# First stage of a two-layer diffusion backbone: by quarters of the features, with two engines' order written out

## The chip, the cores and the metric

The kernel runs on one core of a Trainium2 chip. The metric is the device time of one execution in microseconds (us). Five engines each work through an instruction list of their own: TensorE (PE, matrix products), VectorE (DVE), ScalarE (ACT), GpSimd (POOL) and SyncE (SP), which here issues nearly all loads. They wait for each other through semaphores; a load is done by 16 DMA engines.

## The reference, cut to what matters

The change touches the start of layer 0 alone. There, 768 tokens (512 latent, 256 context) of 1024 features are normalised, shifted and scaled by a modulation that comes from the condition vectors, and projected by one wide matrix:

```python
m_lat = jnp.split((sc @ mod_w[l] + mod_b[l])[:, None, :], 6, axis=-1)      # sc = silu(c)
m_ctx = jnp.split((scc @ mod_w[l] + mod_b[l])[None, None, :], 6, axis=-1)  # scc = silu(c_ctx)
h_ctx = _modulate(_rms(x_ctx, norm_pre_mix[l]), m_ctx[0], m_ctx[1])        # h * (1 + scale) + shift
h_lat = _modulate(_rms(x_lat, norm_pre_mix[l]), m_lat[0], m_lat[1])
gq, gk, gv, gog, gz, aq, ak, av = _split(h @ w_in, EVEN_SIZES)             # 256 256 512 512 32 512 128 128
logit = (z @ gla_w_gate[d] + gla_b_gate[d])                                # z: halves of gz
g = log_sigmoid(logit) / 16                                                # forget gates of the linear attention
```

Parts 0 and 1 of the modulation (shift and scale) are wanted at once. Parts 2 and 3 are wanted after the mixer; parts 4 and 5 later. Then come gated linear attention, attention with rotary positions, an output projection, a feed-forward layer, and a second layer of the same build.

## The kernel before, in words

Every fp32 product is made from three products of a rounded operand H and its remainder L (`mm3`): H·H, H·L and L·H. A weight is loaded to `raw`, rounded by ScalarE into `wH` and subtracted by VectorE into `wL`; the activations get the tiles `x` (H and L) in the same way. Wide tiles of 1024 columns in PSUM (`mm_tile`, two buffers) take projections, 512-column ones (`sc0`, `sc1`, and `tr` with two buffers) take small results and transposes.

The first stage (`run`, L1655 to L1709) loads six token tiles, normalises them, and has TensorE transpose them into `xT` (features on the partitions). Then the modulation's parts 0 and 1 are summed by TensorE in two halves of 512 features: eight loads of 512 KB to a half, 32 products per half (`mod_acc`), a copy (`modrows`), a transpose (`modT`), and a column for each feature (`modcol`, `aff`). With these, VectorE and ScalarE scale `xT` and split it. Only with all 1024 features there does the first projection begin (z and the first half of the attention's queries, 288 columns, tiles `nat`).

After that TensorE's order is written out: `run("qk0 qk0 e m ...")` names generators, and each name advances one of them by a step; `pin` keeps those instructions in that order, while VectorE, ScalarE and SyncE are ordered by the scheduler's own estimates. The names are `qk0` (queries and keys of the linear attention, `gqk0` and `gqk2`), `v0` (its values), `q` (the other half of the attention's queries), `kv`, `e` (the forget gates: z turned to `zT`, products `logit`, then `am` and `glaf`) and `m` (`mod_vec`, L531). A step of `m` loads 512 KB of `mod_w` and has VectorE add it, times a condition value, to two running sums `macc` (latent and context). Eight steps make the pair of part 2, eight more the pair of part 3; each pair ends with `mod_acc` on TensorE (a sum over the partitions), `modrows`, `modT` and `modcol`. Behind these stands the gated linear attention (`c0`, `l0`, tiles `arrg`, `pcg`). Its inputs are `gqk0`, `gqk2` and `glaf`.

Of the kernel before, what the change touches and what calls it, by code (L numbers as in the profile page):

```python
# [17 lines left out]
P = 128  # L18
# [321 lines left out]
class Net:  # L340
# [3 lines left out]
    def __init__(self, ctx, tc, I, out):  # L344
        self.tc, self.nc, self.I, self.out = tc, tc.nc, I, out
        tc.nc.scalar.preload_act_table_set("silu_and_others")
        self.side = 0
        self.whole = False
        self.pinned = False
# [38 lines left out]
    def constants(self):  # L388
# [11 lines left out]
        self.col_rows(  # L400
            "rows", 0, P, (
# [6 lines left out]

        nc.gpsimd.memset(self.scT, 0.0)
        nc.scalar.activation(  # L410
            self.scT[:, :, 0:2].rearrange("p k r -> p r k"),
            self.col[:, R_C : R_C + 16].rearrange("p (r k) -> p r k", r=2),
            AF.Silu,
        )
        self.modcol, self.gates = {}, {}

    def col_rows(self, nm, r0, r1, parts):

        rows = self.wp.tile([P, WU], F32, tag="mraw", bufs=2, name=nm)[: r1 - r0, :P]
        for at, src, n in parts:  # L420
            self.nc.scalar.dma_start(out=rows[at - r0 : at - r0 + n, :], in_=src)
        pt = self.tr_tile(f"pt_{nm}")
        self.tr(pt[:, 0 : r1 - r0], rows, self.ident[0 : r1 - r0, 0 : r1 - r0])
        self.nc.vector.tensor_copy(self.col[:, r0:r1], pt[:, 0 : r1 - r0])

    def late_constants(self):
        nc, I, cst = self.nc, self.I, self.cst
        self.col_rows(
            "rows2", R_NQM, R_END, (
# [10 lines left out]
        mf = self.wp.tile([P, WU], F32, tag="mraw", bufs=2, name="masks_f")[:, :160].rearrange("p (m i) -> p m i", m=5)  # L440
        nc.scalar.dma_start(out=mf, in_=I["const_masks"])
        nc.vector.tensor_copy(self.masks, mf)
# [30 lines left out]
    def mod_loads(self, l, ms, k, pool, bufs):  # L473
        us = []
        for m in ms:
            u = (pool or self.wp).tile([P, WU], F32, tag="mraw", bufs=bufs, name=f"mraw{l}{m}{k}")
# [54 lines left out]
    def mod_vec(self, pool, jobs, own=None, bufs=2, sums=2, single=False):  # L531
# [4 lines left out]
        load = lambda l, k, m: self.mod_loads(l, (m,), k, own, bufs)[0]  # L536
        u = load(*steps[0])
        i = 0
        for l, ms, then in jobs:
            self.mod_tiles(l, [m for m, r in ms if r == 0])  # L540
            accs = [pool.tile([P, D], F32, tag="macc", bufs=sums, name=f"macc{l}{m}{r}") for m, r in ms]
            while i < len(steps) and steps[i][0] == l and steps[i][2] in [m for m, _ in ms]:
                k, m = steps[i][1:]
                i += 1
                ahead = load(*steps[i]) if i < len(steps) else None
                here = [(a, r) for a, (mm, r) in zip(accs, ms) if mm == m]
                for x, (a, r) in enumerate(here):
# [3 lines left out]
                    if k == 0:  # L551
                        nc.vector.tensor_scalar(a, u, w, None, op0=ALU.mult)
                    else:
                        nc.vector.scalar_tensor_tensor(a, u, w, a, op0=ALU.mult, op1=ALU.add)  # L554
                u = ahead
# [63 lines left out]
    def rstd(self, ss, n, w=1, f=1.0):  # L619
        nc = self.nc  # L620
        ms = self.sm.tile([P, w], F32, tag=f"ms{w}", name="ms")
        nc.vector.tensor_scalar(ms, ss, f / n, f * EPS, op0=ALU.mult, op1=ALU.add)  # L622
# [4 lines left out]
    def sumsq(self, src, junk=None, ss=None):  # L627
# [4 lines left out]
        self.nc.scalar.activation(junk, src, AF.Square, accum_out=ss)  # L632
# [55 lines left out]
    def unit(self, src, k, n, pool=None, to=None):  # L688
# [10 lines left out]
        nc.scalar.copy(H[:, :m], raw[:, :m])  # L699
        nc.vector.tensor_tensor(L[:, :m], raw[:, :m], H[:, :m].bitcast(F32), op=ALU.subtract)  # L700
# [357 lines left out]
    def even_mixer(self, h, mix, zu, last):  # L1058
# [14 lines left out]
        gqk = [mixg.tile([P, NT], F32, tag=f"gqk{x}", bufs=1, name=f"gqk{2 * x}") for x in range(2)]  # L1073
        og = [p.tile([P, NTT, 256], F32, name=f"og{c}") for c, p in enumerate((mixg, mix))]
        tp = self.open_pool("gate")
        zn = tp.tile([P, NTT, 32], F32, name="zn")
        zT = tp.tile([32, NT], F32, name="zT")

        def ev_z(t0, pt):
            nc.scalar.copy(zn[:, t0 : t0 + 2, :], pt[:, :, 0:32])  # L1080
            nc.scalar.copy(q_part(0)[:, t0 : t0 + 2], pt[:, :, 32:288].rearrange("p t (m e) -> p t m e", m=4))

        with self.tc.issue_after(last):
            self.gemm_nat(w, 1536, 288, h, tiles, ev_z, us=zu)

# [7 lines left out]
        def decays():  # L1093
            for g in range(0, NTT, 4):
                pt = self.tr_tile("zTp")
                n = min(4, NTT - g)
                for i in range(n):
                    self.tr(pt[0:32, i * P : (i + 1) * P], zn[:, g + i, :], self.ident)
                nc.vector.tensor_copy(zT[:, g * P : (g + n) * P], pt[0:32, : n * P])
            yield  # L1100
            for c in range(2):
                yield from self.gla_gates(mixg, tp, c, zT, wg, fs[c])
# [3 lines left out]
        mods = self.mod_vec(tp, ((0, ((2, 0), (2, 1)), (2, R_NQM)), (0, ((3, 0), (3, 1)), None)), tp, 3, 4)  # L1106

        def nat(c0, evac):

            us = self.nat_units(w, c0, 256, 0) + self.nat_units(w, c0, 256, 1)  # L1110
# [5 lines left out]
        def ev_q(t0, pt):  # L1116
            nc.scalar.copy(q_part(1)[:, t0 : t0 + 2], pt[:, :, :256].rearrange("p t (m e) -> p t m e", m=4))
# [4 lines left out]
        gq, gk, ends = {}, {}, {}  # L1122
        def qk(c):
            Ws = {x: self.unit_cols(w, x * P) for x in (c, c + 2)}
            yield
            for x in (c, c + 2):
                pt = self.mm_tile(f"gqk{x}")
                for g in groups:
                    self.gemm_T(pt, Ws[x], h, (g,))
                    if g is groups[-1]:  # L1130
                        t = gqk[x // 2] if c == 0 else mixg.tile([P, NT], F32, tag=f"gqk{x // 2}", bufs=1, name=f"gqk{x}")
# [732 lines left out]
```

## Time and profile before

| | |
|---|---|
| median of three runs | 1747.95 us (1745.9 to 1750.31) |
| the profiled execution | 1749.34 us, span of its instructions 1747.5 us |
| TensorE busy | 1700.9 us, 97% of the span |
| VectorE, ScalarE, GpSimd busy | 1280.9, 857.8, 74.2 us |
| granted TensorE clock, mean | 0.993 of full speed |
| DMA | 187.23 MB, 107 GB/s over the span |

The span runs from the first to the last instruction, and all times in the rows below count from its start. The page cuts it in 40 slices of 43.7 us; only the first slice has TensorE below nine tenths (six), and only it and the next one have the DMA engines at seven tenths or more:

```profile
PE   6999999999999999999999999999999999999998
DVE  5879658735966979787668658787764678878785
...
PEclk8999999999999999999999999999999999999999
DMA  8731013154322424332234752121114333233333
```

A busy TensorE is not TensorE at its peak: a row of the timeline gives the count of merged instructions, and the distance between the starts of equal rows is what one costs.

### The profile page before, as it was taken

What the parts mean: (1) busy time and instruction counts of PE and PEld (TensorE: products, weight loads), DVE (VectorE), ACT (ScalarE), POOL (GpSimd) and SP (SyncE); (2) the same over time, 40 slices, a digit from 0 to 9 for tenths busy, and PEclk for the clock granted to TensorE, in tenths of its full rate; (3) what the DMA queues carried; (4) which work ended last, traced back from release to release, by engine and by line L of the source; (5) the groups of instructions that cost most, each with busy time, mean ns of one, the idle gap of its engine ahead of it and who ended that gap; (6) DMA issues with size and microseconds to landing.
All of it is one profiled execution on the core that took longest, in us unless ns stands there. A gap on an engine that the chain in (4) does not pass through costs nothing. (4 is left out here: it accounts for less than half of the span.)

```text
span 1747.5 us, 32790 instructions
## 1 busy us (share of the span) xinstructions
PE 1700.9 (97%) x13732; PEld 1526.0 (87%) x13732; DVE 1280.9 (73%) x2036; ACT 857.8 (49%) x1473; POOL 74.2 (4%) x93
## 2 busy tenths in 40 slices
PE   6999999999999999999999999999999999999998
PEld 4889986788999989989998988889898899989997
DVE  5879658735966979787668658787764678878785
ACT  5545557746543333333347336666644664344342
POOL 1004100001000000000001000000000100000000
PEclk8999999999999999999999999999999999999999
DMA  8731013154322424332234752121114333233333
GB/s 318 222 112 39 3 39 107 36 156 139 113 90 73 153 77 156 109 110 61 73 123 143 262 160 63 48 62 50 50 62 133 121 98 108 86 102 106 99 106 120
DMA packets 169647, 187.23 MB, mean 107 GB/s; under 512 B 6262, under 2 KB 140956, under 8 KB 169500
## 3 DMA queue, kind: packets, MB, share of 16 engines
q1 hardware_dynamic: 167568, 181.56, 32.8%
q10 hardware_dynamic: 1932, 3.59, 0.7%
q8 instruction: 107, 1.75, 0.4%
q14 instruction: 40, 0.33, 0.1%
HBM read 175.66 MB, written 9.46 MB: 106 GB/s over the span
## 5 line engine op out<-in xcount | busy, mean ns | idle before, releaser
L371 PE MATMUL nat<-wH,x 128*128 128x256 f32 (+1 forms) x1216 | 229.0, 287 | 0.4 <-issue 0.4
L754 ACT CAST wH<-raw 128x1024 fp32r<-128x1024 f32 x120 | 124.5, 1051 | 197.2 <-PE acc L371 86.2
L700 DVE TENSOR_TENSOR wL<-raw,wH 128x1024 fp32r<-128x1024 f32 (+1 forms) x126 | 151.3, 1206 | 84.3 <-ACT wH L699 83.9
L371 PEld LDWEIGHTS nat<-wH,x 128*128 128x128 f32 x1216 | 193.3, 193 | 3.8 <-ACT y L1329 0.8
L755 DVE TENSOR_TENSOR wL<-raw,wH 128x1024 fp32r<-128x1024 f32 x120 | 145.2, 1221 | 64.9 <-ACT wH L754 64.8
L699 ACT CAST wH<-raw 128x1024 fp32r<-128x1024 f32 (+1 forms) x126 | 128.9, 1038 | 127.8 <-PE nat L371 34.4
L371 PE MATMUL nat<-wL,x 128*128 128x256 f32 (+1 forms) x608 | 173.4, 285 | 0.0
L371 PE MATMUL acc<-wH,gH 128*128 128x512 f32 x440 | 171.8, 390 | 0.0
L371 PE MATMUL acc<-wH,gL 128*128 128x512 f32 x440 | 171.5, 390 | 0.0
L371 PE MATMUL acc<-wL,gH 128*128 128x512 f32 x440 | 171.5, 390 | 0.0
L847 DVE TENSOR_TENSOR y<-y,acc 128x1024 f32<-128x1024 f32 x135 | 115.2, 863 | 37.0 <-PE acc L371 32.8
L554 DVE SCALAR_TENSOR_TENSOR macc<-mraw,scT,macc 128x1024 f32<-128x1024 f32 x98 | 122.6, 1277 | 10.7 <-DMA mraw<-in_mod_w_dram 10.4
L371 PE MATMUL ff<-x,wH 128*128 128x512 f32 (+1 forms) x512 | 127.6, 340 | 0.0
L624 POOL TENSOR_TENSOR rs<-ms,neghalf 128x1 f32<-128x1 f32 (+2 forms) x62 | 58.0, 937 | 1543.2 <-DVE ms L622 1543.1
L371 PEld LDWEIGHTS nat<-wL,x 128*128 128x128 f32 x608 | 117.3, 193 | 0.0
L371 PE MATMUL oproj<-wH,x 128*128 128x512 f32 x320 | 102.5, 397 | 3.2 <-ACT x L1270 3.2
L371 PEld LDWEIGHTS acc<-wH,gL 128*128 128x128 f32 x440 | 82.6, 188 | 17.3
L371 PEld LDWEIGHTS acc<-wH,gH 128*128 128x128 f32 x440 | 82.7, 188 | 16.6
L371 PEld LDWEIGHTS acc<-wL,gH 128*128 128x128 f32 x440 | 82.7, 188 | 16.5
L371 PEld LDWEIGHTS ff<-x,wH 128*128 128x128 f32 x512 | 87.3, 190 | 10.1
L955 ACT COPY qkh<-arr 128x512 f32<-128x512 f32 x112 | 70.1, 642 | 36.3 <-DVE arr L960 32.1
L371 PE MATMUL ff<-x,wL 128*128 128x256 f32 (+1 forms) x256 | 86.2, 337 | 0.0
(344 smaller groups left out, 4047.2 us busy)
## 6 DMA issues: line engine op xcount, KB each, us to landing
mraw<-in_mod_w_dram SPq DMA_DIRECT2D x96, 512.0 KB, 4.8
raw<-in_ffn_w_gate_dram SPq DMA_DIRECT2D x44, 512.0 KB, 3.7
raw<-in_ffn_w_up_dram SPq DMA_DIRECT2D x44, 512.0 KB, 3.8
raw<-in_ffn_w_down_dram SPq DMA_DIRECT2D x44, 512.0 KB, 3.6
raw<-in_odd_w_in_dram SPq DMA_DIRECT2D x40, 512.0 KB, 3.7
raw<-in_even_w_in_dram SPq DMA_DIRECT2D x16, 512.0 KB, 4.6
x<-xr SPq DMA_DIRECT2D x14, 512.0 KB, 2.6
xr<-x SPq DMA_DIRECT2D x14, 512.0 KB, 8.1
```

Source lines behind the costliest of these rows:

```text
L371: return self.pin(self.nc.tensor.matmul(*a, **k))
L554: nc.vector.scalar_tensor_tensor(a, u, w, a, op0=ALU.mult, op1=ALU.add)
L624: nc.gpsimd.tensor_tensor(rs, ms, self.neghalf.to_broadcast([P, w]), op=ALU.pow)
L699: nc.scalar.copy(H[:, :m], raw[:, :m])
L700: nc.vector.tensor_tensor(L[:, :m], raw[:, :m], H[:, :m].bitcast(F32), op=ALU.subtract)
L754: self.nc.scalar.copy(H, f)
L755: self.nc.vector.tensor_tensor(L, f, H.bitcast(F32), op=ALU.subtract)
L847: nc.vector.tensor_tensor(y, y, pt, op=ALU.add)
L955: nc.scalar.copy(qkv[:, :, :, half, :], dst)
```

## The change

The first stage is rewritten around quarters of 256 features (`begin`, new). Of each quarter, the modulation's parts 0 and 1 are loaded (four loads of 512 KB), summed by TensorE into `md` (32 products of 128 columns), turned, and used to scale and split that quarter of `xT`. At once TensorE multiplies that quarter by its rows of the weights for `gqk0`, `gqk2` and the values: three projections are open in PSUM at the same time and grow by a quarter each (both `mm` buffers, both `sc` and one `tr` buffer). Per quarter the order on TensorE is: context tokens of all three, the sums of the next quarter's modulation, latent tokens. z is made by small fp32 products in spare columns of `gqk0`'s PSUM tile (`gates`, 16 products after the second quarter and 16 in the fourth). The attention's first queries get a projection of their own (`Q`, 256 columns).

Within the first stage, VectorE's and ScalarE's instructions are pinned as TensorE's are. The steps of `mod_vec` are pinned too: it loads three steps ahead instead of one, from four buffers instead of three, and its first seven steps are written at the end of the third quarter (three) and in the fourth (two and two). The remaining nine are in the plan as `m`. The late constants go through SP's queue instead of ACT's, ahead of the third quarter's loads, and ScalarE's first table load stands behind its first four loads. A norm's input tiles live in a pool of their own (`xr`), whose buffers the modulation's loads and sums take over.

```diff
-    def mod_vec(self, pool, jobs, own=None, bufs=2, sums=2, single=False):
+    def mod_vec(self, pool, jobs, own=None, bufs=2, sums=2, single=False, tags=("macc", "mraw"), deep=1):
...
-        u = load(*steps[0])
+        us = [load(*x) for x in steps[:deep]]
...
-                        nc.vector.scalar_tensor_tensor(a, u, w, a, op0=ALU.mult, op1=ALU.add)
+                        self.pin(nc.vector.scalar_tensor_tensor(a, u, w, a, op0=ALU.mult, op1=ALU.add))
...
+    def begin_loads(self, pp, q):
+        us = []
+        for i in range(2):
+            u = pp.tile([P, 4, 2, 256], F32, tag="mraw", bufs=5, name=f"mraw0{q}{i}")
+            src = self.I["mod_w"][0, 512 * i : 512 * i + 512, 0:2048].rearrange("(k p) (m f) -> p k m f", p=P, m=2)
+            for m in (1, 0):
+                self.nc.sync.dma_start(out=u[:, :, m], in_=src[:, :, m, 256 * q : 256 * q + 256])
+            us.append(u)
+        return us
+
+    def begin_weights(self, q):
...
+        for at, c0, n in ((0, 0, 128), (128, 256, 128), (256, 512, 256)):
+            nc.sync.dma_start(out=rv[:, :, at : at + n], in_=w[:, :, c0 : c0 + n])
+
+        def split():
+            self.pin(nc.scalar.copy(H, raw))
+            self.pin(nc.vector.tensor_tensor(L, raw, H.bitcast(F32), op=ALU.subtract))
...
+    def begin(self, pp, xr, h, xT, us, ws):
...
+        def columns(q, rows, md):
...
+            for r, tok in ((1, slice(512, 768)), (0, slice(0, 512))):
+                for k in range(ks.start, ks.stop):
+                    x = xT[:, k, tok]
+                    if k % 2:
+                        self.pin(nc.scalar.activation(x, x, AF.Identity, bias=shift[:, r, k : k + 1], scale=A[:, r, k : k + 1]))
+                    else:
+                        self.pin(nc.vector.tensor_scalar(x, x, A[:, r, k : k + 1], shift[:, r, k : k + 1], op0=ALU.mult, op1=ALU.add))
+                H, L = h.hl(ks, tok)
+                self.pin(nc.scalar.copy(H, xT[:, ks, tok]))
+                self.pin(nc.vector.tensor_tensor(L, xT[:, ks, tok], H.bitcast(F32), op=ALU.subtract))
...
+        for q in range(4):
+            if q < 2:
+                us[q + 2] = self.begin_loads(pp, q + 2)
+                split[q + 2] = self.begin_weights(q + 2)
+            if q == 2:
+                mods = self.mod_vec(
+                    xr, ((0, ((2, 0), (2, 1)), (2, R_NQM)), (0, ((3, 0), (3, 1)), None)), xr, 4, 2, tags=("x1", "x0"), deep=3
+                )
+            if q == 3:
+                self.held = True
+                wq = [self.nat_units(I["even_w_in"][0], 1568, 256, half)[0] for half in range(2)]
+                self.held = False
+            across(q, 0, ctx)
+            across(q, 1, ctx)
+            values(q, 4)
+            if q in (1, 2):
+                rows = sums(q + 1, us[q + 1], md)
+            if q == 3:
+                gates(range(4, 8))
+                for _ in range(2):
+                    next(mods)
+            across(q, 0, lat)
+            if q == 0:
+                rows = sums(1, us[1], md)
+            if q in (1, 2):
+                columns(q + 1, rows, md)
+            across(q, 1, lat)
+            if q == 0:
+                columns(1, rows, md)
+            if 1 <= q + 1 < 3:
+                ws[q + 2] = split[q + 2]()
+            values(q, 0)
+            values(q, 2)
+            if q == 1:
+                gates(range(4))
+            if q == 2:
+                for _ in range(3):
+                    next(mods)
+            if q == 3:
+                for _ in range(2):
+                    next(mods)
+        return qk, v, wq, mods, late
...
+        for g in range(4):
+            self.pin(nc.vector.tensor_copy(zT[:, 192 * g : 192 * g + 192], pq[32 * g : 32 * g + 32, 768:960]))
+        nc.scalar.mul(gqk[0], pq[:, :NT], 0.125)
+        nc.scalar.copy(gqk[1], pk[:, :NT])
...
-        run("qk0 qk0 e m qk0 e e v0 qk0 e e m qk0 e e m v0 e e m m q v0 m m v0 m m kv q m m q m q m m m m m m m m m qk1 kv m")
+        run("Q m m Q e e m Q m e e m Q m q e e m q m e e q m m q m kv m kv m m m")
+        for _ in mods:
+            pass
         tp.release()
+        xr.release()
         gp = self.open_pool("gla")
-        run("c0 l0 kv m c0 kv c0 v1 qk1 c0 p p qk1 c0 l0 p qk1 l0 c0 g0 qk1 l0 p c1 p v1 l0 p v1 l0 c1 p v1 l0 c1 l1 g1 g0 c1 g0 r0 c1 l1 r0 g0 l1")
+        run("c0 l0 qk1 kv c0 kv c0 v1 qk1 c0 p p qk1 c0 l0 p qk1 l0 c0 g0 qk1 l0 p c1 p v1 l0 p v1 l0 c1 p v1 l0 c1 l1 g1 g0 c1 g0 r0 c1 l1 r0 g0 l1")
```

How the instructions move is shown at two places. The first is VectorE where z is copied out of PSUM (`zT`), from which the forget gates start. In the list of before, with the sums `macc` of the part-2 pair around it:

```order
L554 SCALAR_TENSOR_TENSOR macc020_691<-mraw023_845,scT_79,macc020_691 128x1024
L554 SCALAR_TENSOR_TENSOR macc021_692<-mraw023_845,scT_79,macc021_692 128x1024
L554 SCALAR_TENSOR_TENSOR macc020_691<-mraw024_918,scT_79,macc020_691 128x1024
L700 TENSOR_TENSOR wL_749<-raw_747,wH_748 128x1024
L1099 COPY zT_466<-zTp_678 32x512
L1099 COPY zT_466<-zTp_684 32x256
L554 SCALAR_TENSOR_TENSOR macc021_692<-mraw024_918,scT_79,macc021_692 128x1024
```

And in the changed list, where `col` and `masks` are the late constants, `lb_tmp` the lower bounds of layer 1, and `wL` the remainders of weights for projections still to come:

```order
L570 SCALAR_TENSOR_TENSOR macc021_710<-mraw025_719,scT_78,macc021_710 128x1024
L570 SCALAR_TENSOR_TENSOR macc020_709<-mraw026_775,scT_78,macc020_709 128x1024
L570 SCALAR_TENSOR_TENSOR macc021_710<-mraw026_775,scT_78,macc021_710 128x1024
L431 COPY col_83<-pt_rows2_854 128x86
L454 CAST masks_278<-masks_f_279 128x160
L464 TENSOR_TENSOR lb_tmp_863<-col_83 128x16
L716 TENSOR_TENSOR wL_1106<-raw_1104,wH_1105 128x1024
L1261 COPY zT_844<-gqk0_338 32x192 x4
L467 TENSOR_TENSOR lb_tmp_863<-col_83,lb_tmp_863 128x2x8 x2
L716 TENSOR_TENSOR wL_1112<-raw_1110,wH_1111 128x1024
```

Before, nine of the pair's 16 sums stand ahead of `zT`. Now 14 do, of which three are shown, with two weight remainders among them and a third right before `zT`; only the eighth step follows.

The second place is TensorE, where the forget gates' products `logit` stand. Before, they stand between two parts of a projection:

```order
L371 MATMUL gqk0_653<-x2_313,wL_643 128x256
L371 MATMUL logit00_723<-zT_466,wg_620 128x256
L371 MATMUL logit01_732<-zT_466,wg_620 128x256
L371 MATMUL gqk2_753<-x0_311,wH_648 128x512
L371 MATMUL gqk2_753<-x1_312,wH_648 128x512
L371 MATMUL gqk2_753<-x0_311,wL_649 128x512
```

Now they stand behind the first tile of the attention's queries (`nat_883`, whose last two products are shown), and the sum over the partitions of the part-2 pair (`mod_acc`) follows at once, ahead of the second tile (`nat_959`):

```order
L370 MATMUL nat_883<-wL_731,x2_324 128x256
L370 MATMUL nat_883<-wH_730,x3_325 128x256
L370 MATMUL logit00_934<-zT_844,wg_858 128x256
L370 MATMUL logit01_943<-zT_844,wg_858 128x256
L370 MATMUL mod_acc_952<-macc020_709,one_81 32x512 x2
L370 MATMUL mod_acc_952<-macc021_710,one_81 32x512 x2
L370 MATMUL nat_959<-wH_724,x0_322 128x256
L370 MATMUL nat_959<-wL_725,x0_322 128x256
```

Before, `mod_acc` of this pair stood behind all eight `logit` products and three more tiles. Now it stands between the second and the third of those products. In the changed program `logit` waits for the four copies `zT`, `mod_acc` for the eighth step's sums, and the transposes behind `nat_959` for the copy `modrows` of `mod_acc`.

## Rows read from the trace of the kernel before

**Rows 1.** Busy time by stretch: start:end, length, busy us (count) by engine, PEclk, DMA share, GB/s

```profile
20.00:30.00 10.00, 7.06 (x84) 3.15 (x83) 6.38 (x19) 5.29 (x11) 0.52 (x1) 0.91 1.06 388
30.00:40.00 10.00, 8.11 (x52) 3.72 (x53) 5.17 (x15) 4.00 (x8) 0.00 (x0) 0.50 0.75 251
...
124.00:151.00 27.00, 27.00 (x403) 25.34 (x402) 26.53 (x77) 17.96 (x45) 13.29 (x8) 1.00 0.25 75
151.00:180.00 29.00, 28.83 (x625) 26.48 (x624) 27.03 (x68) 16.38 (x34) 11.23 (x12) 1.00 0.07 21
```

**Rows 2.** Timeline of TensorE, 8 to 61: start us, us, engine, line, operation, count [idle before]

```profile
8.41 1.92 PE L374 MATMUL xT<-ident,xt 128*128 128x128 f32 x8
...
22.00 2.36 PE L371 MATMUL mod_acc<-mraw,scT 128*32 128x256 f32 x38
...
32.97 1.08 PE L371 MATMUL mod_acc<-mraw,scT 128*32 128x256 f32 x8 [0.27 <-DMA mraw<-in_mod_w_dram]
...
37.63 0.59 PE L371 MATMUL nat<-wH,x 128*128 128x288 f32 x1
...
59.60 0.62 PE L371 MATMUL gqk<-x,wH 128*128 128x512 f32 x2
...
60.29 0.62 PE L371 MATMUL gqk<-x,wH 128*128 128x512 f32 x2
```

**Rows 3.** Timeline of ScalarE and VectorE in the first stage

```profile
4.55 1.06 ACT L632 ACTIVATE junk<-xt 128x1024 bf16<-128x1024 f32 x1 [2.54 <-DMA xt<-in_ctx_dram]
...
24.41 0.42 DVE L485 COPY modrows<-mod_acc 128x256 f32<-128x256 f32 x1 [1.62 <-DMA mraw<-in_mod_w_dram]
...
25.43 0.37 DVE L497 TENSOR_TENSOR modcol<-modT,col 128x4 f32<-128x4 f32 x4 [0.59 <-PE modT L374]
...
30.84 0.81 ACT L1703 ACTIVATE xT<-xT,modcol,aff 128x512 f32<-128x512 f32 x1
...
31.68 0.62 ACT L665 CAST x<-xT 128x512 fp32r<-128x512 f32 x1
...
32.33 0.69 DVE L666 TENSOR_TENSOR x<-xT,x 128x512 fp32r<-128x512 f32 x1 [0.23 <-ACT x L665]
```

**Rows 4.** Timeline of ScalarE, copies behind two neighbouring tiles of a projection

```profile
115.10 0.59 ACT L1117 COPY natq<-nat 128x512 f32<-128x512 f32 x1 [8.33 <-PE nat L371]
...
120.95 0.59 ACT L1117 COPY natq<-nat 128x512 f32<-128x512 f32 x1 [0.39 <-PE nat L371]
```

**Rows 5.** Timeline of VectorE, ScalarE and TensorE, operations that the steps below price

```profile
48.76 1.28 ACT L1104 ACT_TABLE_LOAD   x1 [0.26 <-issue]
...
60.13 0.17 DVE L466 TENSOR_SCALAR nlb<-lb 128x16 f32<-128x16 f32 x1
...
66.74 1.00 DVE L1099 COPY zT<-zTp 32x512 f32<-32x512 f32 x2
...
67.99 1.13 PE L371 MATMUL logit<-zT,wg 32*128 32x256 f32 x4
...
81.59 1.22 DVE L700 TENSOR_TENSOR wL<-raw,wH 128x1024 fp32r<-128x1024 f32 x1
...
81.70 0.78 ACT L1136 COPY gqk<-gqk 128x768 f32<-128x768 f32 x1
...
85.00 0.75 DVE L552 TENSOR_SCALAR macc<-mraw,scT 128x1024 f32<-128x1024 f32 x1
...
93.56 7.25 DVE L554 SCALAR_TENSOR_TENSOR macc<-mraw,scT,macc 128x1024 f32<-128x1024 f32 x6
...
120.85 1.06 PE L371 MATMUL mod_acc<-macc,one 128*32 128x512 f32 x8
```

**Rows 6.** Timeline of VectorE and TensorE where the gated-attention stage begins

```profile
123.72 0.42 DVE L1248 TENSOR_TENSOR arrg<-gqk,glaf 128x256 f32<-128x256 f32 x1
...
128.05 0.36 PE L371 MATMUL nat<-wH,x 128*128 128x256 f32 x1
...
152.60 0.29 DVE L1025 COPY Sg<-pdg 128x128 f32<-128x128 f32 x1 [1.59 <-PE pdg L371]
```

More of the change, by code (lines that the diff above doesn't have):

```diff
@@ L540, in mod_vec @@
             self.mod_tiles(l, [m for m, r in ms if r == 0])
-            accs = [pool.tile([P, D], F32, tag="macc", bufs=sums, name=f"macc{l}{m}{r}") for m, r in ms]
+            accs = [pool.tile([P, D], F32, tag=tags[0], bufs=sums, name=f"macc{l}{m}{r}") for m, r in ms]
             while i < len(steps) and steps[i][0] == l and steps[i][2] in [m for m, _ in ms]:
                 k, m = steps[i][1:]
+                if i + deep < len(steps):
+                    us.append(load(*steps[i + deep]))
                 i += 1
-                ahead = load(*steps[i]) if i < len(steps) else None
+                u = us.pop(0)
                 here = [(a, r) for a, (mm, r) in zip(accs, ms) if mm == m]
@@ L1073, in even_mixer @@
         gqk = [mixg.tile([P, NT], F32, tag=f"gqk{x}", bufs=1, name=f"gqk{2 * x}") for x in range(2)]
+        (pq, pk), pv, wq, mods, late = begun
         og = [p.tile([P, NTT, 256], F32, name=f"og{c}") for c, p in enumerate((mixg, mix))]
         tp = self.open_pool("gate")
-        zn = tp.tile([P, NTT, 32], F32, name="zn")
         zT = tp.tile([32, NT], F32, name="zT")
[L1079 to L1084, printed above, removed]
+        for g in range(4):
+            self.pin(nc.vector.tensor_copy(zT[:, 192 * g : 192 * g + 192], pq[32 * g : 32 * g + 32, 768:960]))
+        nc.scalar.mul(gqk[0], pq[:, :NT], 0.125)
+        nc.scalar.copy(gqk[1], pk[:, :NT])
+        for t0 in tiles:
+            nc.scalar.copy(gv[:, t0 : t0 + 2, 0:256], pv[t0])
+        late()
         wg = tp.tile([32, 2, 256], F32, name="wg")
@@ L1114, in nat, with queries, ev_q @@
                 yield
-        def ev_q(t0, pt):
-            nc.scalar.copy(q_part(1)[:, t0 : t0 + 2], pt[:, :, :256].rearrange("p t (m e) -> p t m e", m=4))
+        def queries(n, us=None):
+            def ev_q(t0, pt):
+                nc.scalar.copy(q_part(n)[:, t0 : t0 + 2], pt[:, :, :256].rearrange("p t (m e) -> p t m e", m=4))
+            return nat(1536 + 32 + 256 * n, ev_q, us)
         def ev_kv(t0, pt):
             nc.scalar.copy(natk[:, t0 : t0 + 2, :], pt[:, :, :256])
-        gq, gk, ends = {}, {}, {}
+        gq, gk, ends = {0: gqk[0]}, {0: gqk[1]}, {}
         def qk(c):
@@ L1707, in run @@
-            zu += self.nat_units(I["even_w_in"][0], 1536, 288, 1)
-            self.late_constants()
+                    self.pin((nc.vector.tensor_copy if hf else nc.scalar.copy)(dst, pt.rearrange("p (k i) -> p k i", k=4)))
+            norm(order[0])
+            norm(order[1])
+            scaled(order[0])
+            for i, t in enumerate(order):
+                if i + 2 < len(order):
+                    norm(order[i + 2])
+                if i + 1 < len(order):
+                    scaled(order[i + 1])
+                turn(t)
+                if i == 1:
+                    finish()
@@ L1710, in ender @@
+            begun = self.begin(pp, xr, h, xT, us, ws)
         def ender(pp, l, m, tiles, xsrc, xdst, nxt, h=None):
```

227 lines of the change are left out of this document (136 added, 91 removed).

## The prediction, put on record before the changed kernel ran

> **What bounds the kernel now.** I read the stretches first. TensorE works 7.06 us of 10 between 20 and 30 and 8.11 between 30 and 40, there at the lower of its two clock levels (0.50, 1.2 GHz), while the DMA engines deliver 388 and then 251 GB/s; from 124 to 151 it is never idle, and VectorE is busy 26.53 of 27 beside it; from 151 to 180 it is 28.83 and 27.03 of 29 [rows 1]. The reader should see a first stage that waits for bytes, and then a stretch where two engines are nearly full at once. The timeline gives the edge: the first product of a projection starts at 37.63 [rows 2]. So at most some 37 us are there to be won, and less, since the bytes are the same. Two marks show where the rewritten part ends. VectorE starts the gated attention (`arrg`) at 123.72, and TensorE starts the second tile of `kv` at 128.05 [rows 6]; by then both programs have done the same products. From about 150 on the two programs' lists are equal. VectorE has no gap worth a word between its mark and 152.60, where it waits 1.59 for TensorE [rows 6].
>
> **Step 1, when products can start.** Loading: 3.1 MB of tokens and 2.1 MB of modulation at 0.388 MB/us [rows 1] take 13.4, from about 3 on: landed at 16.5, and 0.5 MB of weights by 18. Turning: the first tile's squares start at 4.55 [rows 3], its transposes at about 8.1, and six tiles at 1.92 per eight transposes [rows 2] end at 8.1 + 11.5 + some gaps = 20.3. The sums of a quarter are 32 products of 128 columns. 38 of 256 took 2.36 [rows 2], so 32 of half the width lie between 1.0 (by columns) and 2.0 (by count); I take 1.3. They end at 21.6. VectorE's list holds a weight remainder (1.22) ahead of the sums' copy, and that waits for ScalarE's last copy and its cast: 20.5 + 1.05 + 1.2 = 22.7. Then the chain: copy 0.3 (0.42 for twice as wide), transpose about 0.3, columns 0.25 (0.37 for four), scale 0.2, half a context pass on ScalarE 0.5 (0.81 for 512), cast 0.62, remainder 0.69 [rows 3]. Products start at t0 = 25.6, instead of 37.63.
>
> **Step 2, the quarters.** A 512-column triple costs 60.29 - 59.60 = 0.69, so 0.23 each [rows 2]; a tile of 48 products with 256 columns costs 120.95 - 115.10 = 5.85, so 0.12 each [rows 4]. Context part 24 x 0.12 = 2.9; latent part 12 x 0.23 + 24 x 0.12 = 5.6; sums and transpose 1.5: 10.0 per quarter. The 16 small products for z add 0.8 (by the sums' columns) to the second and fourth. The last quarter's bytes land at about 40 with 0.388 MB/us, wanted at 50, so loading is covered; the eight small late loads on SP's queue cost it some 3 us that lie in this cover (without it, the third quarter would start 3 later). ScalarE's first table load, now behind four issues, is over before the 4.55 at which the first tile lets it start, and costs nothing. The last columns' transpose is done at 25.6 + 10.0 + 10.8 + 2.9 + 1.5 + 1.4 = 52.2, and VectorE is through with the last quarter 4.85 later (0.3, 0.2, 0.5, 0.6, 0.7 for the context, then ScalarE's cast of 1024 and VectorE's 1.22 behind it): at 57.0. TensorE ends the fourth quarter at 25.6 + 10.0 + 10.8 + 10.0 + 9.3 = 65.7. Had nothing more to wait, it would then be about 10 us ahead of before.
>
> **Step 3, VectorE's list behind that.** It is in order, and here the change is weak. Six sums: 2 x 0.67 + 4 x 1.21 = 6.2 (0.75 alone with overlap; 7.25 for six) to 63.2; two remainders 2.3 to 65.5; eight sums 9.7 to 75.2; constants 0.5; one remainder 1.15; four copies `zT` at 0.3 (1.00 for the two long ones) to 78.0 [rows 5]. One more remainder to 79.3. The lower bounds need an exponential on ScalarE, which has the copy of `gqk0` (0.78) and the table load (1.28) in front, both behind `zT`: 80.3. Eight tiny operations at 0.17: 81.6. The eighth step, 2 x 1.21: 84.0 [rows 5]. Nothing hides this, since 27 us of VectorE's work start only at 57.0.
>
> **Step 4, TensorE meanwhile.** Behind the fourth quarter ScalarE casts a weight (1.05) and copies `gqk2` (0.78), which frees a PSUM buffer: 67.5. One tile of queries: 73.4. Then `logit` waits for `zT`, 4.6, to 78.0; two of them take 1.1 [rows 5]; then `mod_acc` waits for the eighth step, 4.9, to 84.0. Queued behind it is all the rest: the transposes behind `nat_959` hold VectorE's list in turn, but TensorE is late by then, not VectorE. `mod_acc` 1.1, six tiles 35.1, the six other `logit` 5.1, transposes and copy 0.9, second `mod_acc` with copy and transposes 2.4: kv's second tile at 128.6.
>
> **Step 5, the clock.** In the 11.7 us from 73.4 TensorE works 2.2. Before, it worked 38 products until 24.4 and then in short bursts, and eight sums of the same form that cost 8/38 x 2.36 = 0.50 took 1.08 at 32.97, in a stretch with the clock at 0.50 [rows 1, 2]. So I expect the tile after the wait to begin at the lower level. A whole tile there would lose up to another 5.85; the level comes back within it, and I take a third, so the loss is between 0 and 2.0. The skill has it so too: the Trainium skill, "TensorE: Matmul & The Clock Gate", section "What's actually happening", says that the default state is throttled and that activity releases it. By that rule the full 2.0 would be lost here; the trace agrees with it in rows 1.
>
> **Sum.** TensorE's mark: 128.6 to 130.6 against 128.05, so +0.6 to +2.6. VectorE's mark stands behind the copy of the second `mod_acc`: 128.6 - 1.3 + 0.6 = 127.9 to 129.9 against 123.72, so +4.2 to +6.2; the 1.59 that it waited absorbs a part, and +2.6 to +4.6 stay. Both engines are full until 180, so the later one decides: +3.6, the middle. From 180 on the lists are equal and TensorE bound, and I cost the rest at nothing. The profiled execution took 1749.34 (span 1747.5, 1.84 around it), the sum gives 1752.9 there; it lies 1.4 above the median of the three runs, so against that I forecast 1747.95 + 3.6 = 1751.5.
>
> **Rivals.** (1) Slower: the clock falls already before t0. Between the first sums and the first products TensorE does one transpose in 4 us; if it starts at the lower level, the first quarter costs the same 2.0 more, every mark moves, and some 20 hand-overs between engines at 0.1 to 0.15 that I left out add 2 to 3. That gives +5.6 to +8.6: 1755. For it speaks the same row of the clock (0.50 after a thin stretch); against it that the turning and the sums are dense until 21.6. It decides from 1.6 above my middle. (2) Faster: the turning goes at ScalarE's pace and not at TensorE's. ScalarE needs 1.06 and 0.59 per tile plus a readout, about 1.8, so it could be through at 4.55 + 11 = 16, t0 would be near 21.6, all marks 4 earlier, and with no loss to the clock and VectorE's lateness partly in slack it ends at -4 to -6: 1743. Against it: the transposes' 0.24 each is what a row shows [rows 2], and the waits in step 4 move along, not away. (3) It does not do what it says: 1 KB and 512 B rows load so slowly that quarters wait for bytes. At half the rate of rows 1 the last quarter lands near 70 instead of 40, and the stage ends 15 to 20 later: 1766. Against it: the rate has to fall by a fifth before any quarter is late at all (wanted at 49, landed at 40), and the 388 was reached with rows of 2 KB, no far cry from 1 KB.
>
> **Chances.** The forecast with its own range 1746 to 1753 has 0.50, rival 1 0.31, rival 2 0.15, rival 3 0.04. A measurement of this kernel tells about 0.3%, 5.2 us, from no change. The forecast's bounds lie within it but for a small part; rival 1 lies above it but for a part, rival 2 half below: faster 0.13, same 0.49, slower 0.38. The range, 1742 to 1760, takes in the forecast, rival 1 and nearly all of rival 2, and leaves out rival 3.
>
> **What would show it.** Right: first `gqk` product at 24 to 27; `zT` copies at 76 to 80 with 14 sums ahead without a gap; TensorE idle before `logit` and `mod_acc`, 3 to 6 us each; `arrg` at 127 to 131; a granted clock near 0.5 behind the wait. Wrong: TensorE without those two waits (then it ends some 8 us earlier), or `arrg` before 123, or the quarters waiting for loads. If VectorE's lateness at 150 is 4 and the end is not later at all, the step that both engines are full is the one that failed.

## The result, and the profile after

The changed kernel takes 1756.3 us (median of 14 runs, 1752.17 to 1760.78) beside 1748.09 of the kernel before on the same chip: ratio 1.0045, 95% interval 1.0036 to 1.0055, so 6 to 10 us slower. On a second chip the same pair gave 1.0027 (1.0016 to 1.0037). The forecast was 1751.5 with the range 1742 to 1760. The median moved by 8.2; 3.6 was forecast. The profiled execution took 1756.45, 7.1 more than that of before.

The stretches, with the columns of [rows 1]:

```profile
20.00:30.00 10.00, 7.45 (x94) 6.58 (x94) 6.43 (x11) 5.46 (x7) 0.00 (x0) 0.87 0.78 220
30.00:40.00 10.00, 10.00 (x118) 8.82 (x117) 2.82 (x9) 3.06 (x5) 0.00 (x0) 0.96 1.07 342
50.00:60.00 10.00, 10.00 (x131) 8.77 (x120) 3.38 (x9) 1.94 (x3) 0.00 (x0) 1.00 0.55 182
...
70.00:80.00 10.00, 4.75 (x29) 4.55 (x28) 10.00 (x9) 3.21 (x5) 0.00 (x0) 0.76 0.89 272
80.00:90.00 10.00, 7.92 (x46) 5.83 (x46) 8.61 (x23) 5.05 (x10) 0.00 (x0) 0.84 0.63 199
90.00:100.00 10.00, 10.00 (x62) 7.15 (x56) 2.35 (x8) 1.89 (x4) 0.00 (x0) 0.89 0.16 54
```

Between 30 and 40 TensorE is now full, where it had 8.11 at the lower clock level. The time comes back at 70 to 90: TensorE is idle for 7.3 us, 5.25 of them in the ten in which VectorE is full. And VectorE has two holes of its own, 6.6 us at 50 to 60 and 7.65 at 90 to 100. The reader should see both at once: an engine that others wait for at 75 stood idle at 55.

TensorE's timeline, with the columns of [rows 2]:

```profile
20.71 1.96 PE L370 MATMUL md<-mraw,scT 128*32 128x128 f32 x64
...
25.21 0.38 PE L370 MATMUL gqk<-x,wH 128*128 128x256 f32 x1 [1.80 <-ACT x L1149]
...
64.25 1.51 PE L370 MATMUL gqk<-xT,zw 128*32 128x192 f32 x32
...
76.91 0.58 PE L370 MATMUL nat<-wH,x 128*128 128x256 f32 x1 [5.25 <-ACT gqk L1263]
...
86.84 0.69 PE L370 MATMUL logit<-zT,wg 32*128 32x256 f32 x2 [1.09 <-DMA wg<-in_gla_w_gate_dram]
88.53 3.12 PE L370 MATMUL mod_acc<-macc,one 128*32 128x512 f32 x8 [0.99 <-DVE macc L570]
91.57 0.58 PE L370 MATMUL nat<-wH,x 128*128 128x256 f32 x1
...
134.78 0.36 PE L370 MATMUL nat<-wH,x 128*128 128x256 f32 x1
```

The first products start at 25.21 (25.6 forecast). The row at 134.78 is the second tile of `kv`, 128.05 before [rows 6]: TensorE's mark is 6.7 late. VectorE's rows, then ScalarE's, then those of SP's queue, which issues the loads:

```profile
61.22 1.23 DVE L1150 TENSOR_TENSOR x<-xT,x 128x1024 fp32r<-128x1024 f32 x1 [1.17 <-ACT x L1149]
...
70.74 9.65 DVE L570 SCALAR_TENSOR_TENSOR macc<-mraw,scT,macc 128x1024 f32<-128x1024 f32 x8
...
81.84 1.44 DVE L1261 COPY zT<-gqk 32x192 f32<-32x192 f32 x4
...
87.19 2.47 DVE L570 SCALAR_TENSOR_TENSOR macc<-mraw,scT,macc 128x1024 f32<-128x1024 f32 x2
...
98.34 0.24 DVE L511 TENSOR_TENSOR modcol<-modT,col 128x8 f32<-128x8 f32 x2 [5.29 <-PE modT L373]
...
134.23 0.41 DVE L1427 TENSOR_TENSOR arrg<-gqk,glaf 128x256 f32<-128x256 f32 x1
...
161.40 0.28 DVE L1041 COPY Sg<-pdg 128x128 f32<-128x128 f32 x1
```

```profile
75.11 1.04 ACT L715 CAST wH<-raw 128x1024 fp32r<-128x1024 f32 x1 [11.07 <-DMA raw<-in_even_w_in_dram]
...
76.06 0.79 ACT L1263 COPY gqk<-gqk 128x768 f32<-128x768 f32 x1
```

```profile
45.90 5.70 SPq L713 DMA_DIRECT2D raw<-in_even_w_in_dram  x3
63.80 5.11 SPq L491 DMA_DIRECT2D mraw<-in_mod_w_dram  x3
69.72 1.51 SPq L713 DMA_DIRECT2D raw<-in_even_w_in_dram  x2
```

The last columns end at 62.45, `zT` at 83.3, the eighth step at 89.7, `arrg` starts 10.5 later than in [rows 6], `Sg` 8.8 later. ScalarE's rows explain the 5.25 that TensorE waited at 76.91: ahead of the copy of `gqk2` stands the cast of a weight for `q`, whose load came late. That load was late because of VectorE: on SP's queue it stands behind three loads for the sums, and the first of these waits 12.1, up to 63.80, for a buffer that VectorE's first sums `macc` give back. These are pinned behind the last columns and start at 62.36. From about 192 on the lag of all engines is constant: the first transposes of the feed-forward's input (`hT`) start at 393.9 instead of 386.8, 7.1 later, and the end is as late.

### The profile page after: what moved, and what is told of

Same layout as the page of the kernel before. It is cut to its first block, busy times and chain, and to the rows that moved or that the text cites. A ratio compares the mean times of both kernels' runs of the same rounds, so it can differ in the third digit from the quotient of the medians.

```text
span 1754.7 us, 33160 instructions
## 1 busy us (share of the span) xinstructions
PE 1702.6 (97%) x13918; PEld 1532.6 (87%) x13918; DVE 1282.4 (73%) x2030; ACT 856.7 (49%) x1462; POOL 75.2 (4%) x93
## 5 line engine op out<-in xcount | busy, mean ns | idle before, releaser
L770 ACT CAST wH<-raw 128x1024 fp32r<-128x1024 f32 x120 | 124.5, 1051 | 197.5 <-PE acc L370 86.3
L370 PE MATMUL nat<-wH,x 128*128 128x256 f32 x1120 | 210.2, 287 | 5.3 <-ACT gqk L1263 5.3
L716 DVE TENSOR_TENSOR wL<-raw,wH 128x1024 fp32r<-128x1024 f32 x120 | 146.6, 1228 | 80.1 <-ACT wH L715 79.8
L771 DVE TENSOR_TENSOR wL<-raw,wH 128x1024 fp32r<-128x1024 f32 x120 | 145.1, 1220 | 64.2 <-ACT wH L770 64.0
L370 PEld LDWEIGHTS nat<-wH,x 128*128 128x128 f32 x1120 | 178.3, 194 | 9.4 <-ACT gqk L1263 5.5
L715 ACT CAST wH<-raw 128x1024 fp32r<-128x1024 f32 x120 | 124.1, 1051 | 117.7 <-PE nat L370 27.1
L370 PE MATMUL nat<-wL,x 128*128 128x256 f32 x560 | 159.6, 285 | 0.0
L370 PEld LDWEIGHTS nat<-wL,x 128*128 128x128 f32 x560 | 108.6, 194 | 0.0
```

The costliest lines, as they stand in the source:

```text
L370: return self.pin(self.nc.tensor.matmul(*a, **k))
L715: keep(nc.scalar.copy(H[:, :m], raw[:, :m]))
L716: keep(nc.vector.tensor_tensor(L[:, :m], raw[:, :m], H[:, :m].bitcast(F32), op=ALU.subtract))
L770: self.nc.scalar.copy(H, f)
L771: self.nc.vector.tensor_tensor(L, f, H.bitcast(F32), op=ALU.subtract)
```

## Experiments

Each run is measured against the kernel before on its own chip. There are three chips: one for the copies, the plan, both and the three early steps; one for the changed kernel again, half the sums, both fillings and all with the steps early; one for the rest. The changed kernel stands on one of them only. Its ratio differed by 0.0018 between two chips, so ratios of two chips that are closer than that are not told apart. In the traces the first sums of the modulation start between 18.7 and 20.7; what a run has ahead there is none of its edit's doing.

**The changed kernel again.** No edit.

> The changed kernel as it is, on the chip of the next three, as their measure: 0.3 to 0.5% over the kernel before. In its trace the first quarter may run at the full clock or partly at the lower level; the first query tile waits 5 for ScalarE's copy, and arrg starts at 132 to 135 either way.

1.0027 (1.0016 to 1.0037); last columns at 61.7, `arrg` at 133.10, second `kv` tile at 133.65, `hT` at 392.8. The first sums start at 20.00. The others are compared with these.

**Theory A against theory B.** A: ScalarE's late cast is the loss. B: VectorE's list holds TensorE, whichever wait shows. (As SP's rows show, the late load hangs on VectorE's list too, so A's wait can be B's at one remove.) First the copies and the loads of `wg` are put ahead of the cast, which the last line shown issues:

```diff
+            self.pin(nc.scalar.dma_start(out=wg[16 * d : 16 * d + 16, d, :], in_=I["gla_w_gate"][0, d]))
+        self.pin(nc.scalar.copy(gqk[1], pk[:, :NT]))
+        for t0 in tiles:
+            self.pin(nc.scalar.copy(gv[:, t0 : t0 + 2, 0:256], pv[t0]))
...
+        q1 = [self.nat_units(w, 1824, 256, half)[0] for half in range(2)]
```

> ScalarE's copies out of PSUM (gqk2, the values) and the two wg loads stand ahead of the two casts of weights for q; VectorE's and TensorE's orders stay. Theory A (TensorE's 5.25 us before the first query tile is the loss): the tile starts at 72 to 73 instead of 76.9, and the end is 4 to 5 us earlier than in the changed kernel. Theory B (VectorE's list from 62.4 on holds TensorE: zT at 83, the eighth step at 89.7): the tile starts as early, but TensorE then waits some 5 before logit and 3 to 4 before mod_acc; arrg and the end stay within 1 us of the changed kernel.

Ratio 1.0020 (1.0010 to 1.0030), `hT` at 392.0. TensorE's waits from 60 on (us in total, times, longest):

```profile
PE mod_acc L370 <- DVE macc L570: 3.9, 1, 3.9
PE nat L370 <- ACT gqk L1268: 2.7, 1, 2.7
```

The first wait is halved: the tile starts 2.7 earlier, at 73.5. Of this, 0.8 is left at `hT`, and `mod_acc` waits 3.9 instead of 0.5. The wait moved, which speaks against A; the early-`zT` run takes all of A's wait away.

**The plan alone, and both.**

```diff
-        run("Q m m Q e e m Q m e e m Q m q e e m q m e e q m m q m kv m kv m m m")
+        run("Q m m Q Q e e Q m e e m m q m q m e e q m m e e q m kv m m kv m m m")
```

> Only TensorE's written order behind the first stage is changed: two query tiles ahead of the first logit, mod_acc behind the third tile, and modT behind the next two logit products. The late cast stays. Theory A: the 5.25 stays, so at most the 2 us of the two small waits go. Theory B: with the eighth step no longer waited for, TensorE's mark (second kv tile, 135.0) comes 3 earlier, but VectorE idles as long for mod_acc as before, and the end is 0 to 3 earlier. No gain over 3 by either.

> The edits of the two kernels ahead together. Theory A: as the first alone, 4 to 5 earlier. Theory B: two gates in a row, so more than the sum of the two alone: TensorE has no wait over 1 us before the second mod_acc, arrg at about 128 instead of 134.2, the end 4 to 7 earlier than the changed kernel (0 to 3 later than the kernel before). With less time at the lower clock level behind the wait it gains up to 4 more on TensorE, but VectorE's list is then the later one.

1.0012 (1.0004 to 1.0021) and 1.0010 (1.0001 to 1.0019), `hT` at 391.0 and 390.4. Of their 1.8 and 2.4 against the changed kernel, 1.1 and 0.4 were there before the edits act (last columns 60.6 and 61.25). The large gain of both together, forecast by B, did not come: the first tile still waits 2.8 for the copy of `gqk2`, and a new wait is there (`gcT` for VectorE's `gc`, 2.2).

**zT early.** The four steps of the fourth quarter (two of them from each of two places) behind the copies of z:

```diff
             if q == 3:
                 gates(range(4, 8))
-                for _ in range(2):
-                    next(mods)
...
+        for _ in range(4):
+            next(mods)
```

> The four steps of the fourth quarter stand behind the copies of z (zT) in VectorE's list, so six sums stand ahead of zT instead of 14; the number of sums ahead of mod_acc and TensorE's order stay. If the 14 sums ahead of zT were what holds TensorE: zT at 70 to 73 instead of 81 to 82, and the end 4 to 8 earlier. List theory (the eighth step ahead of mod_acc is the gate, and all 27 us of VectorE's list stand ahead of it in any order): zT as early, logit without a wait for it, but mod_acc still at 88 to 90, and the end within 1 of the changed kernel.

1.0027 (1.0017 to 1.0037), as the changed kernel. `zT` ends at 73.7 and the query tile starts at 71.4 without a wait. TensorE's waits and its stretch:

```profile
PE mod_acc L370 <- DVE macc L570: 9.2, 1, 9.2
```

```profile
80.00:90.00 10.00, 1.71 (x6) 0.38 (x8) 9.33 (x20) 2.10 (x6) 0.00 (x0) 0.52 0.68 203
```

This shows B: the wait that I had forecast for `zT` and the one that I found at the late cast are gone, and all of it stands before `mod_acc`, which starts at 88.29 instead of 87.76.

**Half the sums.** The kernel leaves out half of the features in the sums of quarters 2 to 4.

```diff
+                    if q and k % 4 > 1:
+                        continue
...
```

> The sums of quarters 2 to 4 leave out half of their features (16 products instead of 32), so the modulation of three quarters is incomplete. Each sum takes 1.0 instead of 1.95. List theory: the last columns end 2.5 to 3 earlier (59.6 instead of 62.4), and as VectorE has no gap in the next 27 us, zT, the eighth step and arrg follow by the same, and the end by 2.5 to 3. Rival (TensorE's first wait is set by the late load and not by the stage's length): the first query tile still starts at 76 to 77, and the end gains under 1.

1.0010 (1.0001 to 1.0020). The last columns end at 59.8, 1.9 earlier, `zT` and the query tile 1.9 earlier, `hT` 1.5: the list moves with the stage's end, and the query tile does not stay at 76. But 0.9 of the 1.9 was there before the edit acts (second quarter's sums at 30.12 instead of 31.04). A halved sum takes 1.08 instead of 1.96, so TensorE saves 2.6, and 1.0 of it comes through. At the third sums TensorE now waits 1.4 for the copy `modrows`; ahead of that copy VectorE waits 3.1 for ScalarE's cast of a weight. Up to 62 ScalarE's casts wait 4.9 for such loads in two places (longest 3.2), where the changed kernel there waits 2.1 in two. So behind the sums stand the loads.

**The clock.** Extra products in both of TensorE's waits: 2 and 7 around the first `columns`, 18 behind the transpose of `rows2`; then those of the first wait alone:

```diff
...
+        for _ in range(7):
+            self.mm(fill[:, 0:128], self.ident, self.ident, start=True, stop=True)
...
```

> Extra products of 128 columns that nobody reads fill TensorE's two waits: 9 between the first sums and the first quarter's products (0.24 each), 18 behind the transpose of the late constants, where it waited 5.25. Clock theory (the lower level behind these waits is a loss of its own): the query tile takes 5.9 instead of 8.2 and mod_acc 1.1 instead of 3.1, the first quarter loses nothing, kv's second tile and the end come 4 to 6 earlier. List theory (VectorE's list gates TensorE at mod_acc until 89.7): the query tile is quicker, but logit and mod_acc then wait longer by as much; only what mod_acc and the tile behind it lost comes back, 2 to 3, and up to 2 where the first quarter had run at the lower level.

> Of the extra products only the 9 between the first sums and the first quarter's products. If the 5 us that the kernel with both fillings lost at the end came from the second filling: the end is within 1.5 of the changed kernel, or up to 1.5 earlier where the first quarter would have run at the lower level. If any extra products at the start cost it: 3 to 6 later than the changed kernel again, with the marks up to 390 not later.

The first quarter, with the first filling alone:

```profile
20.00:30.00 10.00, 9.33 (x128) 8.03 (x121) 5.72 (x10) 4.03 (x5) 0.00 (x0) 1.00 0.81 224
```

The clock stays up, and from the first sums to the second it takes 9.87 instead of 11.04. Of this 1.2, 0.4 is left at the fourth sums; ScalarE's casts wait 3.9 for weights up to 62, instead of 2.1. The last columns end at 60.05, 1.6 earlier than in the changed kernel, but the first sums began 1.3 earlier, which is not the filling's doing. `hT` is 1.5 earlier, the ratio 1.0021 (1.0008 to 1.0033), not to be told from 1.0027 on the other chip.

With both, the query tile takes 6.0 instead of 7.8, so the second filling keeps the clock up as well. Yet `mod_acc` starts just 1.2 earlier, as the eighth step ends 1.3 earlier, and `hT` 0.3: the lower level ahead of the gate cost nothing. The ratio is 1.0058 (1.0044 to 1.0072), the median 5.3 above that of the changed kernel on the same chip: in the profiled execution it takes 1369.8 from `hT` to the end instead of 1360.9, with the same order of instructions on every engine. Of these 8.9, 6.0 are idle time of TensorE. What the 18 extra products have to do with it stays open.

**The order of the sums.** Three steps written ahead of the fourth quarter's sums, instead of at the quarter's end; then all steps without a fixed place on VectorE:

```diff
+            if q == 2:
+                for _ in range(3):
+                    next(mods)
...
-            if q == 2:
-                for _ in range(3):
-                    next(mods)
```

> The first three steps of the sums (6 operations, 6.2 us) stand ahead of the fourth quarter's modrows copy, in the 4.33 us in which VectorE waits there, instead of behind the last columns. Theory B: the whole list is 5 to 6 earlier (zT at 77 to 78, eighth step ended at 84), the late weight's load too, and the end 5 earlier than the changed kernel. Theory A: 4 to 5 too, but only because the late weight's load comes earlier: the first query tile at 72 to 73 and no wait for macc behind it. Against both: the copy of modrows is up to 2 late, or the data of the three steps have not landed by 51, and the last columns' chain moves back as far as the sums came forward: 0.

```diff
-                        self.pin(nc.vector.tensor_scalar(a, u, w, None, op0=ALU.mult))
+                        nc.vector.tensor_scalar(a, u, w, None, op0=ALU.mult)
...
-                        self.pin(nc.vector.scalar_tensor_tensor(a, u, w, a, op0=ALU.mult, op1=ALU.add))
+                        nc.vector.scalar_tensor_tensor(a, u, w, a, op0=ALU.mult, op1=ALU.add)
```

> The sums macc are no longer fixed in VectorE's written order; all else is as in the changed kernel. In its list now four sums stand ahead of the fourth quarter's modrows, four more between the operations of its last columns, and five of the next pair's between the copy of mod_acc and modcol, where VectorE waited 5.0 for modT. List theory: the eighth step ends 5 to 7 earlier, VectorE's idle time at 90 to 100 goes down from 7.3 to under 4, arrg at 124 to 128 instead of 133, the end 5 to 8 earlier. If the fixed order is no loss: within 1. Against it: sums between the last columns' operations delay the fourth quarter's products by 2 to 4, and the end gains under 2.

The first: 0.9996 (0.9987 to 1.0005), `hT` at 387.8, 5.0 earlier (0.9 was there at the first products). SP's wait for the first sums falls from 12.1 to 2.4, so here both the list and the late load come earlier. The second: **0.9965 (0.9952 to 0.9977)**, faster than before, `hT` at 384.3. Its stretches, to be held against those of the changed kernel above, and its sums in the two holes:

```profile
50.00:60.00 10.00, 10.00 (x132) 8.71 (x125) 9.19 (x14) 1.17 (x4) 0.00 (x0) 1.00 0.61 188
...
80.00:90.00 10.00, 10.00 (x68) 7.36 (x66) 9.76 (x23) 4.67 (x11) 0.00 (x0) 1.00 0.73 221
90.00:100.00 10.00, 9.82 (x77) 9.28 (x77) 9.68 (x14) 8.63 (x16) 0.00 (x0) 1.00 0.39 124
```

```profile
51.41 1.41 DVE L568 TENSOR_SCALAR macc<-mraw,scT 128x1024 f32<-128x1024 f32 x2
52.73 2.48 DVE L570 SCALAR_TENSOR_TENSOR macc<-mraw,scT,macc 128x1024 f32<-128x1024 f32 x2
...
83.66 1.41 DVE L568 TENSOR_SCALAR macc<-mraw,scT 128x1024 f32<-128x1024 f32 x2
84.98 3.67 DVE L570 SCALAR_TENSOR_TENSOR macc<-mraw,scT,macc 128x1024 f32<-128x1024 f32 x3
88.57 0.23 DVE L511 TENSOR_TENSOR modcol<-modT,col 128x8 f32<-128x8 f32 x2
```

VectorE's holes of 6.6 and 7.65 shrink to 0.8 and 0.3, `modcol` waits for nothing, though the last columns end later (64.0). SP's wait for the first sums is now at most 4.5. Against the changed kernel, one edit on one engine's order is worth 8.5 us at `hT` (0.62% by the ratios, which are of two chips), and turns the loss into a gain.

The two holes are not worth the same. TensorE from `mod_acc` to the second `kv` tile, with the free sums and then with the three steps early:

```profile
80.69 1.06 PE L370 MATMUL mod_acc<-macc,one 128*32 128x512 f32 x8
81.68 0.39 PE L370 MATMUL nat<-wH,x 128*128 128x256 f32 x1
...
124.87 0.36 PE L370 MATMUL nat<-wH,x 128*128 128x256 f32 x1
```

```profile
85.20 0.58 PE L370 MATMUL nat<-wH,x 128*128 128x256 f32 x1
...
128.56 0.36 PE L370 MATMUL nat<-wH,x 128*128 128x256 f32 x1
```

From the tile behind `mod_acc` to the second `kv` tile it is 43.2 with the second hole filled, and 43.4 with the three early steps, where VectorE still waits 5.4 there for `modT` (42.9 and 43.2 in the two traces of the changed kernel). So the second hole cost TensorE nothing. All is won ahead of that tile: with the free sums the eighth step ends at 77.8 instead of 88.9, and `mod_acc` no longer waits for it. Of these 11.1, 6.1 are there at `zT`; the other 5.0 come behind it: one sum is left there instead of two, and it stands right behind `zT`, no longer behind a weight remainder and the lower bounds.

**A version of all.** The early steps, ScalarE's copies first, and this plan, with the first step of the next pair directly behind `modT` and `gcT` a tile later; then the same with free sums instead of early ones (only the plan is shown):

```diff
...
-        run("Q m m Q e e m Q m e e m Q m q e e m q m e e q m m q m kv m kv m m m")
+        run("Q m m Q e e Q m e e m Q m q m q m e e q m m e e q m kv m kv m m m")
```

> All that the first four runs point to: three steps of the sums in VectorE's wait ahead of the fourth quarter's modrows, ScalarE's copies and the wg loads ahead of the late casts, mod_acc behind the second query tile, modT behind two logit products, the first step of the next pair directly behind modT, and the transposes of gates (gcT) a query tile later. Expected: no wait of TensorE over 2 between 71 and 125; VectorE idle under 4 between 80 and 110 instead of 9; arrg at 122 to 125, kv's second tile at 124 to 127: 8 to 10 earlier than the changed kernel, 0 to 4 earlier than the kernel before. Against it: VectorE's list is full from 62 to 123 with 60 us of work, so what TensorE wins does not show, and the end stays within 2 of the kernel before.

> The kernel with all edits, but instead of three steps written earlier the sums are left free as in the kernel ahead. If the scheduler's place for the sums is as good as the written one: arrg and the second kv tile within 2 of that kernel, ratio to the kernel before 0.995 to 0.998. If the sums between the last columns' operations hurt: 2 to 5 later than that kernel.

0.9965 (0.9953 to 0.9978) and **0.9955 (0.9942 to 0.9967)**, the fastest: 1744.29 beside 1752.26 of before. Between 30 and 130 no wait of TensorE is longer than 0.8 in either. The second `kv` tile of the last one:

```profile
121.74 0.36 PE L370 MATMUL nat<-wH,x 128*128 128x256 f32 x1
```

| kernel | last columns end | zT ends | mod_acc starts | second kv tile | hT starts | ratio |
|---|---|---|---|---|---|---|
| changed, first chip | 62.45 | 83.3 | 88.53 | 134.78 | 393.9 | 1.0045 |
| changed | 61.69 | 82.5 | 87.76 | 133.65 | 392.8 | 1.0027 |
| copies first | 61.61 | 81.3 | 86.55 | 132.83 | 392.0 | 1.0020 |
| zT early | 62.40 | 73.7 | 88.29 | 135.49 | 394.7 | 1.0027 |
| half the sums | 59.82 | 80.6 | 85.89 | 132.12 | 391.3 | 1.0010 |
| three steps early | 62.18 | 76.9 | 82.16 | 128.56 | 387.8 | 0.9996 |
| free sums | 64.03 | 76.4 | 80.69 | 124.87 | 384.3 | 0.9965 |
| all, steps early | 62.45 | 76.0 | 84.41 | 122.44 | 381.8 | 0.9965 |
| all, free sums | 63.11 | 75.5 | 83.72 | 121.74 | 381.1 | 0.9955 |

The ratios of the last seven rows are of three chips. `hT` less the second `kv` tile is 259.1 to 259.4 in every row, and 258.8 before: TensorE's mark decides when `hT` starts. VectorE's `arrg` starts 0.5 to 0.6 ahead of that tile in every row, so it follows TensorE's mark too. From there to the end the traces, but for the one with both fillings, take 1360.5 to 1364.3 (1360.7 before), so 4 us at the end can be chance in a single one.

## Why the prediction was right, step by step

The direction and the range held; of the marks named beforehand, few did. The first product came in its place (25.21), and the clock was at 0.50 from 76 to 82, behind the wait. But `zT` ended at 83.3 (76 to 80 named), `arrg` started at 134.2 (127 to 131), and the two waits of 3 to 6 us ahead of `logit` and `mod_acc` were 1.1 and 1.0; a 5.25 stood ahead of the query tile instead.

**Step 1** held: 25.21 for 25.6. **Step 2** was mis-sized, and this is the term that made the forecast too low. The sums take 1.96, not the 1.3 that I chose between 1.0 and 2.0; three of them, 2.0. The z products take 1.51, not 0.8: 1.4. Both have one cause, a misread row: an fp32 product stands in the trace as two records (x64 for the 32 products of a sum, x32 for the 16 of z), so the 38 of [rows 2] are 19 products. By columns, 64 records of 128 at 2.36 / (38 x 256) are 1.99, and 32 of 192 are 1.49, as measured. The first quarter ran at the lower level (rival 1's clock fall): 11.07 from its sums to the next, against 9.6 in the two executions that stayed at 1.00, so 1.4. Together 4.8 of the 6.3 that TensorE took longer from the first product to the fourth quarter's end (71.65 instead of 65.7); the rest is not priced. The last columns end at 62.45 instead of 57.0. Two smaller slips: the parts named for the last quarter add up to 4.6, not 4.85, and the trace has 5.2; the eight late loads hold SP's queue from 21.44 to 28.56, not for 3 us. The cover that I saw for the loads is thin: up to 62 ScalarE's casts wait 0.8 for weights in the first trace, but 4.8 in the run with the new plan, where the first quarter was quicker. The Trainium skill, "FP8 and Floating Point Precision", section "TensorE Precision Notes", has true fp32 as four passes through the array. At 0.23 per 512 columns [rows 2] and with the four column groups of a sum side by side, 32 x 4 x 128 columns make an estimate of 1.84 by that rule; the trace agrees with its 1.96.

**Step 3** held to the letter as a length: from the last columns to the end of `zT` I had 21.0, and the trace has 20.8 in all six executions with that list. It stood 5.4 later. "Nothing hides this" was true of the order as written; that the order itself was the fault, with VectorE idle for 6.6 us just ahead, I did not see.

**Step 4** had the two waits at the wrong places and nearly the right end. The 4.6 for `zT` did not show, since the late cast held the tile before it; I had that cast begin at 65.7, and it began at 75.1, behind the load that VectorE's sums held up. The early-`zT` run shows that it changes nothing: `mod_acc` waits for the eighth step in any case (84.0 forecast, 89.7 measured). The Trainium skill, "PSUM — Partial Sum Buffer", section "Engine vs sequencer instructions", says that the queues of ScalarE and VectorE are strict FIFO; ScalarE's 11.07 ahead of the copy agrees (in the early-`zT` run, without that cast in front, the same copy runs at 68.69). Behind `mod_acc`, 43.5 was forecast to the second `kv` tile and 43.2 measured. I wrote that the hold of VectorE by `modT` does no harm, as TensorE is the late one. That held: it left VectorE its second hole of 7.65, and with the hole filled TensorE takes the same 43.2.

**Step 5**: the tile behind the wait took 8.2 instead of 5.9, a little over the 2.0 forecast; it lay ahead of the eighth step and cost nothing, as the second filling shows. Behind the gate the level cost at least 0.9: from the end of the eighth step to the next tile 1.9, where `mod_acc` at the full clock takes 1.0 (free sums).

**The sum** failed in its last rule. VectorE's mark was 10.5 late, TensorE's 6.7, and the end 7.1: VectorE's lateness beyond TensorE's is taken up by 192 but for 0.4, so TensorE's mark decides, not the later one. I let VectorE's decide, less 1.59. The two errors, a mark 5 too early and the wrong mark, partly cancel, and so 3.6 was nearer to 7.1 than the working deserved; that the result lies within the range is in part luck. Rival 1 had the right sign and time (1755) and the right place for 1.4 us of the gap; the hand-overs that it added to get there were not measured apart.

## What to carry to other kernels

Fixing an engine's order fixes its idle time too: before sums of 1.2 us are pinned in a list, look at where that engine waits and put them there, or leave them free. Only idle time ahead of an instruction that others wait for is worth filling: of the two holes here, the one of 6.6 ahead of `mod_acc` counted, the one of 7.65 behind it did not. An engine that is 73% busy over the span can be the bound for 30 us; find the one instruction that all waits stand before, and test it by removing the waits ahead of it: if they only move on, it is the gate. A pinned list also holds the loads whose buffers it frees, and through them engines that never read its results.

## What the runs showed of the hardware that was not expected

With the same written order up to there, the first quarter's granted clock fell to 0.50 (1.2 GHz) in nine executions without extra products and stayed at 1.00 in two (the new plan, and both). The mean from 20 to 30 was 0.71 to 0.87 in the nine, though TensorE was busy for 3.2 to 3.6 of the 6 us from 20 in all eleven. From the first sums to the second it took 11.0 to 12.1 in the nine and 9.6 in the two. With 9 extra products there it was 1.00 in both executions that had them.

An fp32 product stands in the trace as two records, before (128 records `mod_acc` for 64 products) as after (256 of `md` for 128), and it costs by columns of both. And 18 extra products at 72 us, with all orders equal, went with 9 us more between 390 and the end in the one trace, 5.3 in the medians; this is not explained.
